# GpSimd's large operations given to VectorE and ScalarE in a hybrid recurrent layer; ScalarE evicts every channel tile

## The chip, the cores and the metric

The kernel runs on one core of a Trainium2 chip. The metric is the time of one execution in microseconds of device time. Three runs of the kernel before took 653.14, 647.74 and 653.92 us; the median is 653.14 us.

## What is computed

One decoder layer is applied to a prompt of 1024 tokens and to a sample group of 64 tokens (8 sequences of 8), 1088 token columns in all. The input is projected once, `z = x @ w_in` (1024 wide), and the columns of z feed four branches of width 256 each:

```
A  RG-LRU:          causal conv of width 4, two sigmoid gates, h = a*h + sqrt(1-a^2)*(gate*x)
B  Mamba-2 SSD:     conv, SiLU, chunked scan, + D*x, gated RMSNorm
C  Gated DeltaNet:  conv, SiLU, l2-normed q and k, triangular solve per chunk, state per chunk, RMSNorm
D  S5:              16 groups of a 64-dim complex diagonal state, GELU, GLU
mix = concat(A, B, C, D), each times its SiLU gate
y   = LayerNorm(alpha * x + mix @ w_out) = (v - mean) * rstd * ln_g + ln_b
```

The outputs are y and the new states of the branches. All values are fp32; the large products are built from a high and a low part of each operand, so that every product is three matmuls.

## The kernel before

The token columns lie on the free axis, channels on the 128 partitions. Engines: TensorE (PE) does matmuls and transposes, VectorE (DVE, `V` in the code, with `tt`, `ts`, `stt` for its operations), ScalarE (ACT, `act`), GpSimd (POOL, `G`), SyncE (SP) issues nearly all DMAs. The kernel is written with generators: `merge` mixes streams by weights, and a planner of the framework then lays down, at compile time, the order of the instructions on each engine. It mostly follows the order of the text, and lets a later instruction pass where an earlier one would still be waiting. On the chip each engine works through its own order.

The stages, in the order of the text:

- `u_tiles` splits x into high and low parts and projects S5's input; `gemm_tok` (from L391) projects the token-wise columns: per 128 tokens 24 matmuls into a bank, ScalarE's eviction (L403), ScalarE's tanh, VectorE's L407 and a DMA of the result to DRAM (L408).
- `s5` (L448) works in two halves, `hf` 0 and 1, of four state pairs each. For each half: `table` (L623) builds powers of the unit rotation by doubling, seven steps of a complex multiplication `cmul` (L455, lines 463 to 465) that is six operations; `outs` (L610) builds the output weights `lo` with six operations on 128x512 (L618 to L620); `half_run` (L636) multiplies the chunk sums by the table (two `cmul` of 128x512), runs eight scans (L650), forms the states `H`, and has TensorE apply `lo` to `H` (L676) and the lag matrix to the inputs (L672). `table(0)` runs on VectorE; `table(1)` and both `outs` run on GpSimd. The temporaries `cm` share four buffers between VectorE and GpSimd.
- Channel tiles of 128 channels: `gemm_strip` (L246) loads a weight tile, ScalarE rounds its high part (L156), VectorE forms the low part (L157), and `gemm_block` (L221) makes three blocks of token columns, 24 matmuls each (L226 to L228), into one of two banks of the pool `pg`. `copy_out` (L239) evicts a block: three calls of four go to ScalarE (L242), the fourth to VectorE (L244). Then `conv` on VectorE (L266) and SiLU (L276 to L279), and GpSimd's small copies of the tails (L270, L271).
- From about 205 us two streams run merged: `gdn` (chunks of 128 tokens: `prep` L787, `invert` L828, `state`, `finish` L990) and `side` (RG-LRU, SSD, the gates, then `project`). In `invert` six levels alternate TensorE (L855, L862, L867), VectorE (L857 and the copies L846 of `spread`) and ScalarE (L864, L868). GpSimd does the decayed keys `kd` (L801), the low part `al` (L839), the decay of the sample states (L966, L1177), SSD's skip `D*x` (L1095), and the square in RG-LRU (L1211).
- `project` (L1382): per 128 tokens two halves of 24 matmuls (L1426 to L1428), VectorE adds alpha*x (L1429) and takes statistics (L1430 to L1435), GpSimd takes the root (L1437), ScalarE normalizes (L1442), GpSimd multiplies by `ln_g` and adds `ln_b` (L1443, L1444, 1024 columns each), and a DMA stores the tile. The last of the nine token tiles takes another way, on VectorE alone (L1448, L1450).

Of the kernel before, what the change touches and what calls it, by code (L numbers as in the profile page):

```python
# [13 lines left out]
AF = mybir.ActivationFunctionType  # L14
OP = mybir.AluOpType
# [37 lines left out]
def hybrid_step(ctx, tc, I, O, dbg=None):  # L53
# [182 lines left out]

    flip = [0]

    def copy_out(dst, src):  # L239
        flip[0] += 1  # L240
        if flip[0] % 4:
            act(dst, src, AF.Copy)  # L242
        else:
            V.tensor_copy(dst, src)  # L244

# [202 lines left out]
    def s5(dp):  # L448
# [161 lines left out]
        def outs(hf):  # L610
# [5 lines left out]
            for j, (u, v) in enumerate((((pa[0], ce[0]), (pa[1], ce[1])), ((pa[0], ce[2]), (pa[1], ce[0])))):  # L616
                x, y = (dt_("cm").rearrange("p (a b c) -> p a b c", a=4, b=8) for _ in range(2))
                G.tensor_tensor(x, *u, OP.mult)  # L618
                G.tensor_tensor(y, *v, OP.mult)
                G.tensor_tensor(lo[:, j], x, y, OP.subtract)  # L620
            return lo.rearrange("p r q t i -> p r q (t i)")

        def table(hf):  # L623

            q0 = 4 * hf
            tab = strip(dp, name="tab")[:, :1024].rearrange("p (r q c) -> p r q c", r=2, q=4)
            for j in range(2):
                (V if hf == 0 else G).tensor_copy(tab[:, j, :, 0], u8[:, j, q0:q0 + 4])
            s = 1
            while s < P:  # L630
                cmul(tuple(tab[:, j, :, s:2 * s] for j in range(2)), tuple(tab[:, j, :, 0:s] for j in range(2)),
                     tuple(tab[:, j, :, s - 1:s].to_broadcast([P, 4, s]) for j in range(2)), [4, s], *((V, V) if hf == 0 else (G, G)))
                s *= 2
            return tab[:, 0], tab[:, 1]
# [105 lines left out]
    def h4(z):  # L740
        return z.rearrange("p (h d) -> p h d", h=4)
# [20 lines left out]
    def gdn(wk, up, q, k, v, rk, rq):  # L762
# [24 lines left out]
        def prep(ti):  # L787
# [12 lines left out]
            kd = r1("kd", "vk", 3)  # L800
            G.tensor_tensor(h4(kd[:n]), h4(kh[:n]), bc(ed[:n, ti], 64), OP.mult)  # L801
            gam = gammas(wk, ti, ac, nac, HO, "i", "g", 2)
# [25 lines left out]
        def invert(d):  # L828
# [9 lines left out]
            for s in blocks:  # L838
                G.tensor_tensor(al[s, :, s], A[s, :, s], ah[s, :, s], OP.subtract)  # L839

# [64 lines left out]
        def state(d):  # L905
# [46 lines left out]
            if ti == 0:  # L952
                for hp in range(2):
# [7 lines left out]
                    for hh in range(2):  # L961
# [3 lines left out]
                        mm(ps[hh * 64:hh * 64 + 64], kd[:NS, h * 64:(h + 1) * 64], wm[:NS].rearrange("p b v -> p (b v)"), start=True, stop=True)  # L965
                    G.tensor_tensor(S0[hp], S0[hp], bc(els, 64), OP.mult)  # L966
                    tt(S0[hp], S0[hp], ps.rearrange("p (b v) -> p b v", b=8), OP.add)
# [73 lines left out]
    def ssd(wk, up, x, BT, CT):  # L1041
# [17 lines left out]
        def chunk(ti):  # L1059
# [34 lines left out]
            y = r1("y")  # L1094
            G.tensor_tensor(h4(y)[:n], h4(xt)[:n], bc(hv[:n, 16:20], 64), OP.mult)  # L1095
            tt(y[:n], py[:n, :256], y[:n], OP.add)
# [68 lines left out]
        def sample_state(bt, xw, st):  # L1165
            for g in range(2):
# [9 lines left out]
                mm(ps, xw[:NS, g * P:(g + 1) * P], bm[:NS].rearrange("p b n -> p (b n)"), start=True, stop=True)  # L1176
                G.tensor_tensor(st[:, g], st[:, g], bc(els, 64), OP.mult)  # L1177
                tt(st[:, g], st[:, g], ps.rearrange("p (b n) -> p b n", b=8), OP.add)
# [8 lines left out]
    def rglru(wk, up, xc, out):  # L1187
# [9 lines left out]
        for i in range(2):  # L1197
# [12 lines left out]
            q = strip(up, name="aq")  # L1210
            G.tensor_tensor(q[:, :CL], a_[:, :CL], a_[:, :CL], OP.mult)  # L1211
            stt(r[:, :CL], q[:, :CL], 1.0, r[:, :CL], OP.add, OP.mult)
# [169 lines left out]
    def project():  # L1382
# [18 lines left out]
        for i in range(9):  # L1401
# [37 lines left out]
            if i < 8:  # L1439
                nb = small([P, 1], name="nb")  # L1440
                stt(nb[:n], mv[:n, 0:1], -1.0, rs[:n], OP.mult, OP.mult)
                act(y[:n], y[:n], AF.Identity, bias=nb[:n], scale=rs[:n])  # L1442
                G.tensor_tensor(y[:n], y[:n], lnp[0][:n], OP.mult)  # L1443
                G.tensor_tensor(y[:n], y[:n], lnp[1][:n], OP.add)  # L1444
                nc.sync.dma_start(dst, y[:n])
# [87 lines left out]
```

## Time and profile before

| what | value |
|---|---|
| runs | 653.14, 647.74, 653.92 us |
| the profiled execution, its own time | 648.38 us |
| its span, first to last instruction | 646.5 us |
| mean granted TensorE clock | 0.976 of full speed |
| TensorE busy | 589.7 us (91%) |
| VectorE busy | 469.6 us (73%) |
| ScalarE busy | 271.6 us (42%) |
| GpSimd busy | 180.9 us (28%) |

The span is what the trace covers; the execution's own time is 1.9 us more. Busy time of an engine is the union of its instructions, waits excluded. The rows further below are of this one execution.

### The profile page before, as it was taken

To read this page: it belongs to the slowest core of one execution; us is meant where nothing else is said; L and a number is where in the kernel's file an instruction comes from. 1 tells how busy PE (TensorE), PEld (TensorE's weight loads), DVE (VectorE), ACT (ScalarE), POOL (GpSimd) and SP (SyncE) were. 2 spreads that over 40 slices of the span, in tenths; PEclk is the share of its full clock that TensorE was granted. 3 is DMA by queue.
4 is the path that set the end of the run, shared out by engine and by line. 5 is a ranking of instruction groups with operands and counts; after the bars stand their busy time and mean duration, and the time that the engine had idled before them with its cause. 6 is when DMAs were issued, how large, how long until landed. Compare 5 with 4: busy or idle time off the path is not lost.

```text
span 646.5 us, 11718 instructions
## 1 busy us (share of the span) xinstructions
PE 589.7 (91%) x4284; PEld 504.0 (78%) x4284; DVE 469.6 (73%) x1378; ACT 271.6 (42%) x677; POOL 180.9 (28%) x305
## 2 busy tenths in 40 slices
PE   3999699499999999988999999999999796999995
PEld 3999699499999786777888877778777564778884
DVE  5996963782559676899897777868777897754443
ACT  5544235143345244854644434354443752333210
POOL 8313119400101322331502032032030122443633
PEclk9999799889899999999999999999999997999998
DMA  8462113032311010100122021001022511013131
GB/s 288 165 191 63 41 34 86 1 96 59 128 57 55 18 36 33 33 18 19 33 69 68 33 89 66 1 17 43 9 75 78 171 43 49 33 55 113 66 117 78
DMA packets 23929, 44.11 MB, mean 68 GB/s; under 512 B 3073, under 2 KB 10193, under 8 KB 23873
## 3 DMA queue, kind: packets, MB, share of 16 engines
q1 hardware_dynamic: 23696, 42.71, 20.1%
q8 instruction: 33, 0.54, 0.4%
q0 software_dynamic: 176, 0.67, 0.3%
q14 instruction: 24, 0.19, 0.1%
HBM read 32.97 MB, written 10.41 MB: 67 GB/s over the span
## 4 chain that ended last, share of the span: by engine, by line
PE 66%; DVE 19%; POOL 5%; issue 5%; ACT 2%; DMA 1%; SPq 0%; DVEq 0%; ACTq 0%; POOLq 0%
PE pg L226 8%; PE pg L227 8%; PE pg L228 8%; PE pg L1428 5%; PE pg L1427 5%; PE pg L1426 5%; DVE tb L846 2%; DVE yb L846 2%; DVE acc L266 2%; PE ssq L755 1%; PE pg L398 1%; DMA x<-in_x_t_dram 1%; PE pg L399 1%; PE pg L400 1%; PE kq L817 1%
## 5 line engine op out<-in xcount | busy, mean ns | idle before, releaser
L226 PE MATMUL pg<-xh,wh 128*128 128x384 f32 (+1 forms) x432 | 150.2, 348 | 9.0 <-DVE z L244 9.0
L227 PE MATMUL pg<-xl,wh 128*128 128x384 f32 (+1 forms) x432 | 149.0, 345 | 0.0
L228 PE MATMUL pg<-xh,wl 128*128 128x384 f32 (+1 forms) x432 | 147.0, 340 | 0.0
L226 PEld LDWEIGHTS pg<-xh,wh 128*128 128x128 f32 x432 | 82.8, 192 | 12.5 <-DVE z L244 9.3
L227 PEld LDWEIGHTS pg<-xl,wh 128*128 128x128 f32 x432 | 82.6, 191 | 2.1 <-issue 0.5
L228 PEld LDWEIGHTS pg<-xh,wl 128*128 128x128 f32 x432 | 82.4, 191 | 1.3 <-issue 0.3
L1426 PE MATMUL pg<-woh,wh 128*128 128x512 f32 (+1 forms) x144 | 58.2, 404 | 1.9 <-ACT wh L1415 1.9
L1427 PE MATMUL pg<-wol,wh 128*128 128x512 f32 (+1 forms) x144 | 58.5, 406 | 0.2
L1428 PE MATMUL pg<-woh,wl 128*128 128x512 f32 (+1 forms) x144 | 57.9, 402 | 0.4 <-DVE wl L1416 0.4
L266 DVE SCALAR_TENSOR_TENSOR acc<-z,pcol,acc 128x1112 f32<-128x1112 f32 x36 | 49.6, 1381 | 5.1 <-ACT acc L264 4.8
L864 ACT ACTIVATE XY<-XY 128x256 f16<-128x256 f32 (+1 forms) x51 | 19.4, 381 | 53.8 <-PE XY L862 48.2
L156 ACT ACTIVATE wh<-wr 128x512 fp32r<-128x512 f32 (+1 forms) x40 | 25.2, 633 | 35.0 <-PE pg L227 28.3
L1429 DVE SCALAR_TENSOR_TENSOR y<-y,pg 128x512 f32<-128x512 f32 (+1 forms) x18 | 12.3, 686 | 32.2 <-PE pg L1428 28.4
L1426 PEld LDWEIGHTS pg<-woh,wh 128*128 128x128 f32 (+1 forms) x144 | 26.6, 184 | 8.9 <-ACT wh L1415 2.2
L1428 PEld LDWEIGHTS pg<-woh,wl 128*128 128x128 f32 (+1 forms) x144 | 26.6, 185 | 7.3 <-DVE wl L1416 0.9
L1427 PEld LDWEIGHTS pg<-wol,wh 128*128 128x128 f32 (+1 forms) x144 | 26.5, 184 | 7.2 <-DVE wol L1393 1.0
L157 DVE TENSOR_TENSOR wl<-wr,wh 128x512 fp32r<-128x512 f32 (+1 forms) x40 | 28.2, 704 | 2.8 <-ACT wh L156 2.4
L857 DVE TENSOR_TENSOR T<-T,lev 128x256 f16<-128x256 f32 (+1 forms) x51 | 21.4, 419 | 10.7 <-PE T L855 10.1
L868 ACT ACTIVATE XY<-XY 128x256 f16<-128x256 f32 (+1 forms) x51 | 19.4, 381 | 22.5 <-PE XY L867 22.5
L242 ACT ACTIVATE z<-pg 128x384 f32<-128x384 f32 (+2 forms) x37 | 14.0, 389 | 34.5 <-PE pg L228 33.2
L846 DVE COPY tb<-T 64x256 f16<-64x256 f16 x99 | 26.2, 264 | 1.6
L846 DVE COPY yb<-XY 64x256 f16<-64x256 f16 x99 | 23.8, 240 | 4.4 <-ACT XY L868 3.0
(453 smaller groups left out, 1398.0 us busy)
## 6 DMA issues: line engine op xcount, KB each, us to landing
wr<-in_w_tiles_dram SPq DMA_DIRECT2D x40, 256.0 KB, 2.9
x<-in_x_t_dram SPq DMA_DIRECT2D x8, 544.0 KB, 6.3
wo<-in_w_out_dram SPq DMA_DIRECT2D x16, 256.0 KB, 2.9
y<-in_x_dram SPq DMA_DIRECT2D x8, 512.0 KB, 3.3
out_y_dram<-y SPq DMA_DIRECT2D x7, 512.0 KB, 2.6
bgd<-bg SPq DMA_DIRECT2D x9, 128.0 KB, 1.8
dud<-us SPq DMA_DIRECT2D x2, 544.0 KB, 4.2
U<-dud SPq DMA_DIRECT2D x16, 68.0 KB, 3.4
```

Of the source, the lines that this page charges most:

```text
L156: act(hv_, wv, AF.Copy)
L157: lo_eng[0].tensor_tensor(lv, wv, hv_.bitcast(F32), OP.subtract)
L226: mm(o, whi[k], xh[:, k, a:b], start=(k == 0), stop=False)
L227: mm(o, whi[k], xl[:, k, a:b], start=False, stop=False)
L228: mm(o, wlo[k], xh[:, k, a:b], start=False, stop=(k == 7))
L266: stt(acc[:, :CL], s[:, j:j + CL], col(wkey, j * nt + i), acc[:, :CL], OP.mult, OP.add)
L846: V.tensor_copy(dst[s, :, s], src[s])
L857: tt(t_[:n], pt[:n], lev[:n, l].unsqueeze(1).to_broadcast([n, 4, 64]), OP.mult)
L864: act(XY[:n, :256], px[:n, :256], AF.Copy)
L1426: mm(ps[:n], mh[k_], woh[:, k_, e], start=(k_ == 0), stop=False)
L1427: mm(ps[:n], mh[k_], wol[:, k_, e], start=False, stop=False)
L1428: mm(ps[:n], ml[k_], woh[:, k_, e], start=False, stop=(k_ == 7))
```

## The change

`copy_out` always uses ScalarE. Operations of GpSimd go to VectorE: S5's output weights and the second half's table, the low part `al`, the two decays of the sample states, and LayerNorm's multiplication and addition, in halves of 512 columns. Others go to ScalarE: the decayed keys `kd` and the skip `D*x`, each as four `Copy` activations of 64 columns with a scale per partition in place of one operation on 256 columns, and the square of RG-LRU. GpSimd keeps the small powers (L999, L1130, L1437), memsets, masks and tail copies. No DMA is added or taken away.

```diff
     def copy_out(dst, src):
-        flip[0] += 1
-        if flip[0] % 4:
-            act(dst, src, AF.Copy)
-        else:
-            V.tensor_copy(dst, src)
+        act(dst, src, AF.Copy)
...
     # s5, outs
-                G.tensor_tensor(x, *u, OP.mult)
-                G.tensor_tensor(y, *v, OP.mult)
-                G.tensor_tensor(lo[:, j], x, y, OP.subtract)
+                tt(x, *u, OP.mult)
+                tt(y, *v, OP.mult)
+                tt(lo[:, j], x, y, OP.subtract)
...
     # s5, table
-                (V if hf == 0 else G).tensor_copy(tab[:, j, :, 0], u8[:, j, q0:q0 + 4])
+                V.tensor_copy(tab[:, j, :, 0], u8[:, j, q0:q0 + 4])
...
-                     tuple(tab[:, j, :, s - 1:s].to_broadcast([P, 4, s]) for j in range(2)), [4, s], *((V, V) if hf == 0 else (G, G)))
+                     tuple(tab[:, j, :, s - 1:s].to_broadcast([P, 4, s]) for j in range(2)), [4, s])
...
     # gdn, prep
-            G.tensor_tensor(h4(kd[:n]), h4(kh[:n]), bc(ed[:n, ti], 64), OP.mult)
+            for h in range(4):
+                act(h4(kd)[:n, h], h4(kh)[:n, h], AF.Copy, scale=ed[:n, ti, h:h + 1])
...
     # gdn, invert
-                G.tensor_tensor(al[s, :, s], A[s, :, s], ah[s, :, s], OP.subtract)
+                tt(al[s, :, s], A[s, :, s], ah[s, :, s], OP.subtract)
...
     # gdn, state, and likewise ssd, sample_state
-                    G.tensor_tensor(S0[hp], S0[hp], bc(els, 64), OP.mult)
+                    tt(S0[hp], S0[hp], bc(els, 64), OP.mult)
...
     # ssd, chunk
-            G.tensor_tensor(h4(y)[:n], h4(xt)[:n], bc(hv[:n, 16:20], 64), OP.mult)
+            for h in range(4):
+                act(h4(y)[:n, h], h4(xt)[:n, h], AF.Copy, scale=hv[:n, 16 + h:17 + h])
...
     # rglru
-            G.tensor_tensor(q[:, :CL], a_[:, :CL], a_[:, :CL], OP.mult)
+            act(q[:, :CL], a_[:, :CL], AF.Square)
...
     # project
-                G.tensor_tensor(y[:n], y[:n], lnp[0][:n], OP.mult)
-                G.tensor_tensor(y[:n], y[:n], lnp[1][:n], OP.add)
+                for e in (slice(0, 512), slice(512, 1024)):
+                    tt(y[:n, e], y[:n, e], lnp[0][:n, e], OP.mult)
+                    tt(y[:n, e], y[:n, e], lnp[1][:n, e], OP.add)
```

## Rows read from the trace of the kernel before

**Rows 1.** The page, part 1: busy time, share, instructions.

```profile
PE 589.7 (91%) x4284; PEld 504.0 (78%) x4284; DVE 469.6 (73%) x1378; ACT 271.6 (42%) x677; POOL 180.9 (28%) x305
```

**Rows 2.** Waits of TensorE: waiter, releaser: total us, times, longest us.

```profile
PE pg L226 <- DVE z L244: 9.0, 1, 9.0
PE XY L862 <- DVE yb L846: 6.6, 5, 5.0
PE pg L398 <- ACT bg L403: 5.8, 1, 5.8
...
PE XY L867 <- ACT XY L864: 0.4, 2, 0.2
```

**Rows 3.** Stretches: length, busy us (instructions) of each engine, granted clock, DMA.

```profile
72.10:76.00 3.90, 3.90 (x17) 3.90 (x18) 3.90 (x12) 1.45 (x7) 0.00 (x0) 0.51 0.10 34
...
129.70:134.50 4.80, 4.78 (x16) 4.78 (x17) 4.80 (x11) 0.29 (x2) 0.00 (x0) 0.55 0.00 0
...
265.00:345.00 80.00, 74.45 (x613) 64.70 (x612) 71.05 (x161) 45.83 (x102) 21.70 (x43) 1.00 0.11 35
...
538.70:546.00 7.30, 7.29 (x47) 5.44 (x48) 4.33 (x15) 1.53 (x4) 0.00 (x0) 0.67 0.36 108
...
572.00:640.00 68.00, 66.78 (x287) 53.48 (x285) 27.40 (x80) 15.28 (x41) 32.31 (x18) 1.00 0.23 85
```

**Rows 4.** Timeline, VectorE, 50 to 90 us: start, length, operation, [idle <-releaser].

```profile
51.79 0.23 DVE L628 COPY tab<-u 128x4 f32<-128x4 f32 x2
...
60.78 1.17 DVE L465 TENSOR_TENSOR tab<-cm,cm 128x256 f32<-128x256 f32 x1
64.39 1.53 DVE L463 TENSOR_TENSOR cm<-tab,G 128x512 f32<-128x512 f32 x1 [2.43 <-POOL lo L620]
...
69.36 0.41 DVE L407 SCALAR_TENSOR_TENSOR bg<-bg 128x256 f32<-128x256 f32 x1
```

**Rows 5.** Timeline, GpSimd, 88 to 142 us.

```profile
96.02 0.31 POOL L628 COPY tab<-u 128x4 f32<-128x4 f32 x2
```

**Rows 6.** Timeline, VectorE, 88 to 142 us.

```profile
117.15 1.53 DVE L463 TENSOR_TENSOR cm<-tab,G 128x512 f32<-128x512 f32 x1 [10.38 <-POOL lo L620]
...
128.65 0.68 DVE L465 TENSOR_TENSOR H<-cm,cm 128x512 f32<-128x512 f32 x1
...
134.98 0.68 DVE L157 TENSOR_TENSOR wl<-wr,wh 128x512 fp32r<-128x512 f32 x1
```

**Rows 7.** Timeline, TensorE, 128 to 147 us.

```profile
129.72 0.69 PE L226 MATMUL pg<-xh,wh 128*128 128x384 f32 x1 [8.96 <-DVE z L244]
...
135.96 0.63 PE L672 MATMUL y<-U,tz 128*128 128x136 f32 x4
...
141.16 0.42 PE L226 MATMUL pg<-xh,wh 128*128 128x320 f32 x1
```

**Rows 8.** Waits of ScalarE.

```profile
ACT z L276 <- DVE hs L465: 12.9, 1, 12.9
```

**Rows 9.** Timeline, GpSimd, 524 to 572 us.

```profile
533.57 2.33 POOL L1443 TENSOR_TENSOR y<-y,ln 64x1024 f32<-64x1024 f32 x1 [1.54 <-ACT y L1442]
```

**Rows 10.** Timeline, VectorE, 524 to 572 us.

```profile
533.49 2.51 DVE L846 COPY tb<-T 64x256 f16<-64x256 f16 x2
...
541.38 0.46 DVE L846 COPY yb<-XY 64x256 f16<-64x256 f16 x2
```

**Rows 11.** Groups by form, VectorE: shapes, count, busy us, mean ns.

```profile
L463 DVE TENSOR_TENSOR cm<-bk 128x512 f32<-128x512 f32 x4 | 2.7, 684 | 0.0
...
L892 DVE TENSOR_TENSOR x<-XY,F 64x256 f32<-64x256 f16 x8 | 3.3, 412 | 0.1
```

**Rows 12.** Groups by form, ScalarE.

```profile
L944 ACT ACTIVATE qd<-ks,ea 128x64 f32<-128x64 f32 x28 | 6.5, 311 | 1.0 <-DVE R L941 1.0
...
L242 ACT ACTIVATE z<-pg 128x256 f32<-128x256 f32 x3 | 1.1, 377 | 0.0
```

**Rows 13.** Groups by form, GpSimd.

```profile
L801 POOL TENSOR_TENSOR kd<-kh,ed 128x256 f32<-128x256 f32 x8 | 7.2, 906 | 42.7 <-DVE kh L798 15.6 <-DVE oss L997 13.7 <-DVE R L941 13.3
```

More of the change, by code (lines that the diff above doesn't have):

```diff
@@ L235, in gemm_ch @@
             yield 3.7
-    flip = [0]
     def copy_out(dst, src):
-        flip[0] += 1
-        if flip[0] % 4:
-            act(dst, src, AF.Copy)
-        else:
-            V.tensor_copy(dst, src)
+        act(dst, src, AF.Copy)
     def gemm_strip(c0, key, i, pool):
@@ L1176, in sample_state @@
                 mm(ps, xw[:NS, g * P:(g + 1) * P], bm[:NS].rearrange("p b n -> p (b n)"), start=True, stop=True)
-                G.tensor_tensor(st[:, g], st[:, g], bc(els, 64), OP.mult)
+                tt(st[:, g], st[:, g], bc(els, 64), OP.mult)
                 tt(st[:, g], st[:, g], ps.rearrange("p (b n) -> p b n", b=8), OP.add)
```

## The prediction

> **What bounds the kernel now.** The page's first part comes first: TensorE is busy 91% of the span, VectorE 73%, ScalarE 42%, GpSimd 28% [rows 1]. TensorE bounds, so only what takes away its idle time or its lowered clock moves the end; GpSimd's busy time by itself buys nothing. TensorE's own waits are therefore the second view. Apart from the start of the kernel, three of them are long: 9.0 us for VectorE's eviction L244, 5.0 of 6.6 us for the copies `yb`, 5.8 us for ScalarE's `bg` [rows 2]. Behind each of them the granted clock is at the lower of its two levels (1.2 GHz of 2.4) for a while: 3.9 us at a mean of 0.51, 4.8 us at 0.55, 7.3 us at 0.67 [rows 3]. That is 1.9, 2.2 and 2.4 us lost on top, so the three places cost 7.7, 11.2 and 7.4 us, 26.3 in all.
>
> The timelines tell where each comes from. First place: VectorE waits 2.43 us for GpSimd's `lo` and then runs a product in 1.53 us; L407, whose store frees the `bg` buffer that ScalarE and after it TensorE wait for, stands behind, at 69.36 us [rows 4]. Second place: GpSimd begins the second table at 96.02 us [rows 5]. VectorE idles 10.38 us for its `lo`, runs S5's second half from 117.15 us to the end of `H` at 129.33, and only then comes L244 [rows 6], for which TensorE has waited 8.96 us [rows 7]. Third place: GpSimd's LayerNorm product starts at 533.57 us [rows 9]; a pair of copies that VectorE runs in 0.46 us elsewhere takes 2.51 us there [rows 10], and the next pair lies under GpSimd's addition.
>
> **The second stretch of S5, part by part.** VectorE takes over the table. The first table, on VectorE already, ran from 51.79 to 61.95 us, partly against GpSimd [rows 4]: 10.2 us is the upper end, and I take 8.5, since its last operation took 1.17 us where a 512-column one takes 0.68. The output weights are six operations of 0.684 us [rows 11], 4.1 us. So 12.6 us come onto VectorE, which idled 10.38 us in one piece there. If the table keeps its place, it begins at 96.0; of the 21.1 us until 117.15, at most 10.7 were other work. With all of that in front, S5's run begins at 119.3, with none of it at 108.6. I take 116, nearer to the late end, since convolutions of VectorE lie there and what was not idle in one piece was mostly work. The run itself is 12.2 us, and its first product needs 0.68 and not 1.53, the second likewise: 10.5. `H` is ready at 126.5, 2.8 us sooner.
>
> TensorE no longer waits for L244: ScalarE evicts that block in 0.377 us [rows 12]. The third block starts at 120.8, takes 6.2 less 2.2 us (129.72 to 135.96 [rows 7], at full clock) and ends at 124.8. Next in TensorE's order are the products with `H`, 5.2 us [rows 7], from 126.5 to 131.7. The next weight tile's low part ended at 135.66 [rows 6], 6.3 us after `H`; now 132.8. So the next tile starts at 132.8 in place of 141.16, a gain of 8.4. Late next is VectorE with `H` and the low part. Ends: 0, if the eviction again stands behind something on its new engine; 11.2, all of the place.
>
> **The first stretch.** The 2.43 us of waiting go, and the slowed operations around them; an estimate of the latter is 3.3 us (1.53 to 0.68 in one product, the like in three more). 4.1 us of output weights come in. L407 comes 1.6 us sooner. In the second stretch VectorE sets the time, so TensorE's gain here counts only as far as VectorE is sooner too: 1.6 us, ends 0 and 7.7.
>
> **LayerNorm.** Eight tiles, each four operations of 0.684 us on VectorE, 2.7 us in place of GpSimd's two. In the projection's steady part TensorE works 66.78 of 68 us and VectorE 27.4 [rows 3]; six tiles there add 16.4 us to VectorE, and TensorE's products still cover them. Without the cover each tile would cost its 2.7 us. Tile 0 lies within the last chunks of the delta-rule stream, at the third place: the 5.0 us wait becomes one of about 2.7 us, if the four operations are put ahead of the copies. Gain 2.3; ends 0 and 7.4 (wait and clock). VectorE's four operations wait for ScalarE's normalization, which waits for GpSimd's root; behind them on VectorE are the copies of `spread`, for which TensorE's next level waits.
>
> By the Trainium skill, SBUF — State Buffer, section Who interferes with whom, GpSimd and a VectorE copy contend for one shared port pair, which the first holds for its whole instruction. That is what the 2.51 us beside GpSimd's 2.33 us show; by the rule alone, with both GpSimd operations gone and VectorE's own taken as hidden, this term would be an estimated 4.7 us.
>
> **The smaller moves.** `al`: 17 operations of 64x256; the nearest row has 0.412 us [rows 11], so 7.0 us more on VectorE. It is needed only at the end of `invert`, and TensorE's levels cover it; ends 0 and +7.0. From 265 to 345 us VectorE is the tightest, 71.05 of 80 us busy [rows 3]; about four `al` (1.6 us) come there, and some evictions leave. I take +0.5. The four decays are 2.7 us on VectorE, followed only by a state's store: 0, end +2.7. The remaining evictions, some 17 of 0.377 us, put 6.4 us on ScalarE: 0. The two squares are at most 1.6 us each on ScalarE (four times an eviction of 256 columns): 0, ends 0 and +3.2. `kd` and `D*x`: 9 chunks, eight activations each, 72 of 0.311 us [rows 12], 22.4 us on ScalarE (1.24 per operation where GpSimd took 0.906 [rows 13]). ScalarE's load rises from 42% to about 47%, so only the order can hurt: `kd` takes its wait for `kh` along, 15.6 us in four chunks on GpSimd [rows 13], and behind it on ScalarE stand the evictions of `XY`, for which TensorE's levels wait. TensorE waits 0.4 us for these now [rows 2]. I take +1; ends 0 and +38 (22.4 + 15.6).
>
> **Sum.** -8.4 - 1.6 - 2.3 + 0.5 + 1 = -10.8, call it -11. The profiled execution took 648.4 us, of which the span is 646.5 and 1.9 lie around it; so 637.4. It lies 4.8 us under the median of the three runs, whose spread is 6.2; I add half of the 4.8: **640 us**. Own range of this case: 631 to 647.
>
> **Rivals.**
> *The evictions wait on ScalarE.* In the same stretch ScalarE stood 12.9 us at L276, which needs VectorE's convolution [rows 8]. If the planner puts the moved eviction behind L276, TensorE waits as before, and VectorE, with 12.6 us more against 10.4 idle, gives nothing back. The S5 terms are 0, and the rest is -0.8: 650. For it: the wait is there and ends after L244 did. Against it: eviction and L276 belong to tiles of different age, and in the trace before ScalarE had evictions of the same block in front of L276. The Trainium skill, PSUM — Partial Sum Buffer, section Engine vs sequencer instructions, calls the queues of ScalarE, VectorE and GpSimd strict FIFO; the 12.9 us agree, and by that rule everything placed behind L276 waits as long.
> *ScalarE becomes the gate of the inversion (slower).* The place is `prep` beside `invert`: `kd` in order ahead of `XY`. Its price is up to 38 us; half of it against the -12.3 of the gains leaves +6.7, 657 us. It decides from the point where more than a third of the 38 us falls on TensorE's levels. For it: GpSimd could wait at no cost and ScalarE can't. Against it: ScalarE is idle over half the time, and TensorE has other streams to work on.
> *All three stalls go.* If the planner fills VectorE's gaps from 80 us on, nearly all of the 26.3 us return, less 1.5: 648.4 - 24.8 + 2.4 = 626.
> *The change does nothing*, since GpSimd's time was off the path: the waits of VectorE for `lo` speak against it; it would look like the first rival.
>
> **Chances.** Forecast 0.55, evictions waiting 0.22, slower 0.15, all stalls gone 0.08. The measurement tells about 1% (6.5 us) from no change. Faster: 0.50 of the first and 0.08, 0.58. Slower: 0.14 of the slow case and 0.03 of the waiting one, 0.17. Same: 0.25. The range takes in the first two cases, most of the fast one and the slow one's half price: 624 to 660.
>
> **What would show it.** Right: TensorE's waits for L244 and for `lo`'s followers are gone, and the granted clock near 72 and 130 us stays up; `H` of the second half lands some 3 us sooner; no copy L846 takes over 1 us beside a LayerNorm operation; VectorE near 500 us busy, GpSimd near 70. Wrong: a wait of TensorE at 120 us for ScalarE's L242; waits of L862 and L867 for ScalarE's `XY` in place of 0.4 us; tiles of the projection further apart than now, with TensorE waiting for L1416 or L1429.

## The result: 634.9 us, faster, and the profile after

The changed kernel takes 634.88 us (median of 4 runs, 631.94 to 635.67) where the kernel before takes 653.26 beside it; the ratio is 0.975, 95% interval 0.970 to 0.980. Measured again on another chip it was 0.967 (0.961 to 0.972). Of all executions reported here one is left out of its ratio, one of the six of F1 below, which took 3126 us at full clock. So the change is faster, and a little more than I forecast. The profiled execution took 631.94 us (span 630.1) against 648.38: 16.4 us less, where my sum was 11.

The changed kernel's line numbers are 3 to 6 lower than those of before: L397 is the L403 of before, L401 the L407, L457 to L459 the `cmul`, L612 to L614 `outs`, L238 the eviction, L841 the copies, L1411 the high parts of the projection (L1415 before), L1440 and L1441 LayerNorm's affine part.

First the page's busy line, which answers to [rows 1]: VectorE and ScalarE took over 14.9 and 22.4 us, GpSimd lost 102.

```profile
PE 591.5 (94%) x4284; PEld 503.6 (80%) x4284; DVE 484.5 (77%) x1469; ACT 294.0 (47%) x769; POOL 78.7 (12%) x192
```

The waits of TensorE in the changed kernel, against [rows 2]: the 9.0 us for L244 are gone, the 5.8 us for `bg` are 2.6, the longest for `yb` is 1.5 and no longer 5.0. Two have grown by a microsecond or more: `wh` of the projection (its high parts), 1.9 us before, now 2.9, and the transposes' wait for `y` of the chunked scan (L1131), 0.6 us before, now 2.8 in four pieces; 1.6 us for the gated unit's inputs (L712, L713) are new. ScalarE's `XY` still costs 0.4.

```profile
PE XY L857 <- DVE yb L841: 3.1, 5, 1.5
PE pg L1422 <- ACT wh L1411: 2.9, 1, 2.9
...
PE pg L392 <- ACT bg L397: 2.6, 1, 2.6
...
PE XY L862 <- ACT XY L859: 0.4, 2, 0.2
```

The 1.5 us for `yb` are not at LayerNorm but in the delta-rule stream, at 283 us. Where LayerNorm cost 5.0 us, the longest is 0.44:

```profile
283.57 0.29 PE L857 MATMUL XY<-T,yb 128*128 128x64 f16 x4 [1.48 <-DVE yb L841]
...
535.18 0.29 PE L857 MATMUL XY<-T,yb 128*128 128x64 f16 x4 [0.44 <-DVE yb L841]
```

The same kernel's stretches (length; busy us of PE, PEld, DVE, ACT, POOL; granted clock; DMA), against [rows 3]. The first place still has a lowered clock (0.62); the second and the third run at 1.00; the steady projection has VectorE at 40.66 of 68 us, and its token tiles start 11.2 us apart, as before.

```profile
67.70:72.00 4.30, 4.30 (x24) 4.30 (x25) 4.30 (x15) 1.39 (x7) 0.00 (x0) 0.62 0.09 30
116.00:122.00 6.00, 6.00 (x39) 5.87 (x39) 6.00 (x17) 1.77 (x4) 0.13 (x1) 1.00 0.00 0
...
530.00:540.00 10.00, 9.56 (x86) 7.13 (x84) 9.53 (x34) 4.42 (x15) 0.00 (x0) 1.00 0.24 71
556.00:624.00 68.00, 65.60 (x282) 52.28 (x280) 40.66 (x105) 15.26 (x40) 4.13 (x7) 1.00 0.23 86
```

VectorE's timeline in the first place, against [rows 4]: the product with the table starts 0.7 us sooner, takes 0.69 and not 1.53, and L401, whose store frees the `bg` buffer, comes after two operations of S5's run, where five stood in front of it before.

```profile
63.69 0.69 DVE L457 TENSOR_TENSOR cm<-tab,G 128x512 f32<-128x512 f32 x1
64.29 0.69 DVE L458 TENSOR_TENSOR cm<-tab,G 128x512 f32<-128x512 f32 x1
64.89 0.42 DVE L401 SCALAR_TENSOR_TENSOR bg<-bg 128x256 f32<-128x256 f32 x1
```

VectorE in the second place, against [rows 5, 6]. The table starts at 99.08 and S5's run at 110.36, with nothing but S5's own work and one low part (L157) between; `H` is complete at 120.6 (129.3 before), and the first half of the next weight tile's low part is ready eleven microseconds ahead of it. The second half comes at 125.01, 5 us behind `H`.

```profile
99.08 0.24 DVE L622 COPY tab<-u 128x4 f32<-128x4 f32 x2
...
109.16 0.68 DVE L157 TENSOR_TENSOR wl<-wr,wh 128x512 fp32r<-128x512 f32 x1
109.76 0.68 DVE L614 TENSOR_TENSOR lo<-cm,cm 128x512 f32<-128x512 f32 x1
110.36 0.68 DVE L457 TENSOR_TENSOR cm<-tab,G 128x512 f32<-128x512 f32 x1
...
119.91 0.69 DVE L459 TENSOR_TENSOR H<-cm,cm 128x512 f32<-128x512 f32 x1
...
125.01 0.68 DVE L157 TENSOR_TENSOR wl<-wr,wh 128x512 fp32r<-128x512 f32 x1
```

TensorE there, against [rows 7]: the products with `H` follow the channel blocks without a gap, and the next tile starts at 126.32 (141.16 before).

```profile
121.12 0.63 PE L666 MATMUL y<-U,tz 128*128 128x136 f32 x4
...
126.32 0.41 PE L226 MATMUL pg<-xh,wh 128*128 128x320 f32 x1
```

ScalarE evicts the blocks of that stretch at once, none behind the SiLU of [rows 8]:

```profile
112.95 0.50 ACT L238 ACTIVATE z<-pg 128x64 f32<-128x64 f32 x2 [1.33 <-PE pg L228]
117.14 0.49 ACT L238 ACTIVATE z<-pg 128x384 f32<-128x384 f32 x1 [3.69 <-PE pg L228]
```

VectorE at LayerNorm's first tile, against [rows 9, 10]: its own affine operations, 0.68 us each and the first two in one piece, alternate with the copies of `spread`, and every pair of copies takes about 0.46 us.

```profile
524.55 1.28 DVE L1440 TENSOR_TENSOR y<-y,ln 64x512 f32<-64x512 f32 x2
525.76 0.47 DVE L841 COPY yb<-XY 64x256 f16<-64x256 f16 x2
526.25 0.42 DVE L852 TENSOR_TENSOR T<-T,lev 128x256 f16<-128x256 f32 x1
526.60 0.68 DVE L1441 TENSOR_TENSOR y<-y,ln 64x512 f32<-64x512 f32 x1
527.20 0.45 DVE L841 COPY tb<-T 64x256 f16<-64x256 f16 x2
```

**Where the time goes, place by place.** The table gives the start of the same TensorE matmul in every profiled execution, as the difference to before in us, read from the timelines: the first and the last token-wise product (L398 of before), the last product with `H` (L676), the last of the gated unit, the last norm product of the channel tiles, the 64th `J` (`J` are the last matmuls of each chunk's inversion, 16 in a chunk), the first product of the first and of the second token tile of the output projection (the 1st and 17th of L1426), the last `J`, the last product of the projection. Each execution starts with an offset of its own (first column).

```
                    tok0   tokN   H      unit   norm   J64    proj0  proj16  Jlast  projN
before              36.4   82.4  141.0  162.5  191.0  376.9  508.8   526.3  556.1  637.9
the change          -0.2   -4.7  -14.8  -12.4   -9.2  -11.4  -10.2    -7.5  -13.4  -16.3
the change, again    0.3   -4.1  -14.3  -12.0  -12.0  -14.3  -13.2   -10.2  -16.1  -19.1
evict alone         -0.2   -0.3   -6.0   -1.9   -0.3    1.4    2.2     3.0    2.9    2.8
S5 alone            -1.6   -5.5  -13.1  -11.4  -11.3  -11.2  -11.2    -9.6   -9.3   -9.3
S5, output weights   0.6   -5.4   -8.2   -8.2   -8.1   -7.9   -7.9    -7.9   -8.3   -8.3
LayerNorm alone      0.5    0.7    0.8    0.8    0.8    0.8    0.8     0.8   -4.9   -6.9
LayerNorm, POOL too -1.8   -1.9   -2.1   -2.1   -2.1   -2.0   -2.0    -2.0   -7.6    3.9
small moves alone    0.9    1.3    1.5    1.5    3.0   -0.9   -0.8     2.5    0.7    0.6
S5 + LayerNorm       1.1   -5.0  -11.0   -8.8   -7.2   -7.0   -7.0    -5.5  -11.1  -13.2
all but evict       -1.3   -5.4  -11.5   -9.0   -7.4  -11.3  -11.2    -7.8  -13.4  -16.4
all but small        1.0   -5.1  -15.2  -13.1  -11.5   -9.8   -8.9    -8.3  -14.0  -16.1
first tile on DVE    1.1   -4.9  -15.1  -12.7  -11.1  -13.4  -10.6   -13.7  -18.3  -22.0
unit's weights too   0.5   -5.5  -15.7  -14.2  -14.5  -17.8   -9.0   -12.6  -17.3  -21.0
```

"The change, again" is F4 below, "LayerNorm, POOL too" G4, and the two last lines G3 and H1. The changed kernel gains 4.5 us in the first place (4.7 less its own offset of 0.2), 10.1 in the second, loses 5.6 of that by 191 us, gains 1.0 through the delta-rule stream, loses 2.7 at the first projection, and gains 8.8 from LayerNorm's first tile to the end, 5.9 of them by the last `J`.

### The profile page after: what moved, and what is told of

It is laid out like the page before. It is cut to its first block, busy times and chain, and to the rows that moved or that the text cites. A ratio compares the mean times of both kernels' runs of the same rounds, so it can differ in the third digit from the quotient of the medians.

```text
span 630.1 us, 11770 instructions
## 1 busy us (share of the span) xinstructions
PE 591.5 (94%) x4284; PEld 503.6 (80%) x4284; DVE 484.5 (77%) x1469; ACT 294.0 (47%) x769; POOL 78.7 (12%) x192
## 4 chain that ended last, share of the span: by engine, by line
PE 52%; DVE 21%; issue 4%; ACT 4%; POOL 2%; DMA 1%; SPq 1%; DVEq 0%; ACTq 0%; POOLq 0%
PE pg L226 6%; PE pg L228 6%; PE pg L227 6%; PE pg L1424 4%; PE pg L1423 4%; PE pg L1422 4%; DVE acc L260 3%; DVE yb L841 2%; DVE T L852 1%; PE ssq L749 1%; DVE tb L841 1%; PE rg L1199 1%; PE cb L1077 1%; DVE wl L157 1%; PE yd L1088 1%
## 5 line engine op out<-in xcount | busy, mean ns | idle before, releaser
L228 PE MATMUL pg<-xh,wl 128*128 128x384 f32 (+1 forms) x432 | 148.5, 344 | 0.0
L1422 PEld LDWEIGHTS pg<-woh,wh 128*128 128x128 f32 (+1 forms) x144 | 26.4, 183 | 10.2 <-ACT wh L1411 3.4
L238 ACT ACTIVATE z<-pg 128x384 f32<-128x384 f32 (+2 forms) x48 | 17.5, 395 | 32.7 <-PE pg L228 31.1
L157 DVE TENSOR_TENSOR wl<-wr,wh 128x512 fp32r<-128x512 f32 (+1 forms) x40 | 27.4, 688 | 4.8 <-ACT wh L156 4.6
L863 ACT ACTIVATE XY<-XY 128x256 f16<-128x256 f32 (+1 forms) x51 | 19.5, 382 | 14.8 <-PE XY L862 14.5
L841 DVE COPY yb<-XY 64x256 f16<-64x256 f16 x99 | 21.8, 221 | 4.5 <-ACT XY L863 2.9
L1425 DVE SCALAR_TENSOR_TENSOR y<-y,pg 128x512 f32<-128x512 f32 (+1 forms) x18 | 12.3, 682 | 15.3 <-PE pg L1424 15.3
L392 PE MATMUL pg<-wh,xh 128*128 128x268 f32 x72 | 21.4, 298 | 2.6 <-ACT bg L397 2.6
```

What stands on the lines that cost most here:

```text
L157: lo_eng[0].tensor_tensor(lv, wv, hv_.bitcast(F32), OP.subtract)
L228: mm(o, wlo[k], xh[:, k, a:b], start=False, stop=(k == 7))
L392: mm(o, xh[:, k, c0:c0 + P], whi[k], start=(k == 0), stop=False)
L841: V.tensor_copy(dst[s, :, s], src[s])
L1422: mm(ps[:n], mh[k_], woh[:, k_, e], start=(k_ == 0), stop=False)
```

## The experiments

My theory: the gain is made in three places, by S5 and LayerNorm leaving GpSimd, and the small moves are worth nothing. The rivals: the eviction alone does the second place; the whole is a general relief of VectorE from GpSimd; the small moves or the eviction hold it back.

**E1, the eviction alone.**

```diff
-    flip = [0]
-
     def copy_out(dst, src):
-        flip[0] += 1
-        if flip[0] % 4:
-            act(dst, src, AF.Copy)
-        else:
-            V.tensor_copy(dst, src)
+        act(dst, src, AF.Copy)
```

> Of the change only the eviction is made: ScalarE evicts all channel tiles; S5, LayerNorm and the small moves stay on GpSimd. Theory of three places: the third block of the second stretch no longer waits 9 us for L244, but the products with H still wait for H at 129.3 us, so the next weight tile starts about 5 us sooner (136 instead of 141.2); the first and the third place stay as they were. About 643 us in a profiled run of 648, a ratio near 0.992. Rival, the eviction alone made the gain of the second stretch: the whole 10 us, ratio 0.984. Rival, S5 alone made it: ratio 1.000.

Measured: 1.0022 (0.9996 to 1.0048), no gain. TensorE, in this kernel's timeline, runs its third block without a wait and then stands for `H`, as expected:

```profile
127.84 0.50 PE L670 MATMUL y<-H,lo 64*128 64x136 f32 x4 [2.69 <-DVE H L459]
129.22 0.50 PE L670 MATMUL y<-H,lo 64*128 64x136 f32 x4 [0.88 <-DVE H L459]
```

The next tile is 6.0 us sooner, and all of it is gone 50 us later: TensorE waits 2.0 us for the gated unit's rounded weights and inputs, and then runs from 150 to 170 us at a granted clock of 0.85 (its stretch):

```profile
150.00:170.00 20.00, 18.03 (x107) 17.25 (x106) 6.79 (x14) 9.58 (x20) 0.25 (x2) 0.85 0.15 61
```

So the first expectation held up to 141 us and failed after it.

**E2, S5 alone** (output weights and second table on VectorE, the diff of `outs` and `table` that stands ahead).

> Of the change only S5 is made: output weights and second table on VectorE. Every fourth channel tile is still evicted by VectorE; LayerNorm and the small moves stay on GpSimd. Theory of three places: the first place returns its 4.7 us, H comes near 121 us, and what is left of the second place is that the eviction of one block still stands behind S5's run on VectorE, about 3 us; 4.7 + 7, of which about 5 are given back by the gated unit's weights at 141 us and by a lowered clock between 150 and 180 us: about 641, ratio 0.989. Rival, the eviction alone made the gain of the second stretch: only the first place returns, and VectorE's longer list delays the eviction: 645, ratio 0.995 to 1.00.

Measured: 0.9845 (0.9809 to 0.9882), the largest single part. `tokN` -5.5, `H` -13.1, of which 11.3 stay up to the first projection and 9.3 to the end. With VectorE still evicting every fourth tile, TensorE no longer waits for L244; what is left in that place is this:

```profile
PE y L676 <- DVE H L465: 1.9, 1, 1.9
```

So S5's edit alone gives 3.9 of the 4.5 us of the first place (its offset of -1.6 taken out) and 7.6 of the 10.1 us of the second. My expectation that some 3 us of the wait for the eviction would stay was wrong.

**E3, LayerNorm alone** (its product and addition on VectorE, in halves).

> Of the change only LayerNorm's product and addition are made by VectorE, in halves; all else stays as before. Theory of three places: the pairs of copies at 533 and 541 us go back to 0.46 us each, TensorE's wait of 5.0 us for them goes, and so does the stretch of lowered clock: 7.4 to 8.8 us, about 640, ratio 0.987, and nothing differs up to 510 us. Rival, my prediction's sum: 2.3 us, ratio 0.996, since VectorE's four operations stand in front of the copies. Rival, the projection pays for VectorE's longer list: the tiles after 560 us come over 7.0 us apart.

Measured: 0.9877 (0.9832 to 0.9921). Nothing differs until 526 us, then 7.7 us are gained by the last projection. The stretch that holds it, in the kernel before and in this one: TensorE 9.97 and 13.74 of 15 us busy, clock 0.77 and 1.00.

```profile
530.00:545.00 15.00, 9.97 (x65) 7.19 (x64) 11.47 (x31) 3.42 (x7) 5.39 (x3) 0.77 0.18 54
```

```profile
530.00:545.00 15.00, 13.74 (x117) 9.44 (x117) 13.99 (x52) 5.93 (x16) 0.72 (x1) 1.00 0.19 54
```

**E4, the small moves alone** (`al` and decays to VectorE; `kd`, `D*x` and the square to ScalarE).

> Of the change only the small moves are made: al, the states' decays on VectorE; kd, D*x and the gate's square on ScalarE. S5, LayerNorm and the evictions stay as before. Theory of three places: nothing, ratio 0.998 to 1.002; the waits of L862 and L867 for ScalarE's XY stay near 0.4 us. Rival, GpSimd's instructions slow VectorE everywhere and freeing it is worth some microseconds all over the delta-rule stream: ratio 0.992 to 0.995, with the gain growing steadily from 260 to 500 us. Rival, ScalarE's kd holds up the inversion: ratio 1.003 or more.

Measured: 0.9938 (0.9910 to 0.9966), a gain that I had not expected; the profiled execution, 648.75 us, is one of the longest of its twelve (644.4 to 649.5), so its trace shows less than the times. It gains 3.9 us between the norms and the 64th `J`, in one place rather than steadily. From 260 to 300 us, in the kernel before and in this one (VectorE 36.42 and 34.95 of 40 us, TensorE 35.37 and 38.54), and GpSimd less (12.58 and 7.92):

```profile
260.00:300.00 40.00, 35.37 (x266) 30.14 (x265) 36.42 (x79) 25.96 (x50) 12.58 (x26) 1.00 0.09 28
```

```profile
260.00:300.00 40.00, 38.54 (x299) 32.97 (x298) 34.95 (x78) 30.80 (x60) 7.92 (x23) 1.00 0.09 28
```

One of the moved operations can be seen to hold VectorE there. In the kernel before, a pair of copies lies beside GpSimd's square (L1211) and takes 2.19 us; in E4, with the square on ScalarE, the pair of the same place takes 0.45:

```profile
281.65 2.08 POOL L1211 TENSOR_TENSOR aq<-acc 128x1112 f32<-128x1112 f32 x1
281.62 2.19 DVE L846 COPY tb<-T 64x256 f16<-64x256 f16 x2
```

```profile
282.08 0.45 DVE L847 COPY tb<-T 64x256 f16<-64x256 f16 x2
```

And it gives 3.3 us back at the first projection, where TensorE now waits 4.0 us for ScalarE (1.9 us in the kernel before):

```profile
PE pg L1428 <- ACT wh L1417: 4.0, 1, 4.0
```

**F1 to F4, the parts in company**, on one chip: S5 and LayerNorm; the change without its eviction; without its small moves; the change itself.

> S5 and LayerNorm go to VectorE as in the change; the eviction by turns and the small moves stay as before. Theory of two places: the gains of the two single edits add up, 0.9845 x 0.9877 = 0.972, about 632 us, as fast as the whole change. Rival, the second place needs the eviction too: 637 or more. Rival, the small moves carry their own 0.6% in any company: 0.972, and the kernels that have them are 4 us faster than this one.

> The change without its eviction: VectorE still evicts every fourth channel tile, all else as in the change. Theory: the single edits multiply, 0.9845 x 0.9877 x 0.9938 = 0.966, some 5 us under the whole change, since the eviction alone was 1.0022. Rival, the second place needs the eviction: slower than the whole change by 3 us or more, TensorE waiting for L244 near 120 us. Rival, the small moves gain nothing once S5 and LayerNorm are moved: 0.972, the same as without them.

> The change without its small moves: al, kd, D*x, the decays and the gate's square stay on GpSimd; S5, LayerNorm and the eviction as in the change. Theory that the single edits multiply: 0.9745 to 0.975, some 4 us slower than the whole change if that is measured at 0.969, from the stretch between 200 and 510 us. Rival, my prediction's sum (the small moves at +1.5 us): 1 to 2 us faster than the whole change.

> The changed kernel itself again, beside its parts on one chip. The product of the four single edits is 0.9845 x 0.9877 x 0.9938 x 1.0022 = 0.968; the first measurement gave 0.975 (0.970 to 0.980). If it comes near 0.975 again, the parts do not add up, and some 4 us of their gains are lost when they are put together.

Measured, in this order: 0.9705 (0.9658 to 0.9752), 0.9690 (0.9650 to 0.9730), 0.9718 (0.9682 to 0.9754), 0.9668 (0.9614 to 0.9721). S5 and LayerNorm together give what the whole gives; the eviction and the small moves move it by 0.5% at most, less than the intervals. The product of the four single edits, 0.968, lies in the interval of the second measurement and just under that of the first, so nothing shows a loss in putting them together. The traces tell more than the times. Between the norms and the first projection (`norm` and `proj0` of the table) the small moves gain 3.8 us in both kernels that have them without the eviction; the eviction costs 2.5 and 2.6 in both that have it without them; with both, the change's two executions gain 1.0 and 1.2 (G3 and H1, which have both as well, lose 0.5 and 5.5; for H1 see there). Between the first and the seventeenth projection the executions with the small moves lose 2.7 to 3.4, those without them 0 to 1.6 (but for the two last lines, which mend that place). And the eviction's own gain is in the second place (`tokN` to `H`): 10.1 to 10.2 us with S5's edit and the eviction, 6.0 to 7.6 with S5's edit and without it. Each of the two gives back most of what it gains.

**G2, half of S5's edit**: both output weights on VectorE, the second table still on GpSimd.

```diff
-                G.tensor_tensor(x, *u, OP.mult)
-                G.tensor_tensor(y, *v, OP.mult)
-                G.tensor_tensor(lo[:, j], x, y, OP.subtract)
+                tt(x, *u, OP.mult)
+                tt(y, *v, OP.mult)
+                tt(lo[:, j], x, y, OP.subtract)
```

> The kernel before with one half of the S5 edit: both output weights on VectorE, the second table still on GpSimd. Theory: the first place needs only the output weights, since its table was on VectorE already, so the token-wise products end 4 to 5 us sooner, as with the whole S5 edit; in the second place GpSimd begins its table where it did and has only that to make, so VectorE waits less long for it, and part of the rest returns: 642 to 646 where the whole S5 edit gave 0.9845. Rival, the first place moved for another reason (a start that differs from run to run): the token-wise products end where they did.

Measured: 0.9878 (0.9833 to 0.9923). The first place is whole (-5.4 at `tokN`, -6.0 against its own start); the second returns 2.8 of 7.6 us. VectorE now waits for the table, and TensorE for L244:

```profile
105.78 0.69 DVE L618 TENSOR_TENSOR cm<-bk,s5p 128x512 f32<-128x512 f32 x1 [4.45 <-POOL tab L465]
```

```profile
PE pg L226 <- DVE z L244: 5.7, 1, 5.7
```

**G4, LayerNorm on VectorE, and GpSimd busy beside it.** As E3, with two operations of GpSimd per tile whose result is not used.

```diff
+        spare = strip(up, name="spare")[:, :1024]
...
+                G.tensor_tensor(spare[:n], lnp[0][:n], rs[:n].to_broadcast([n, 1024]), OP.mult)
+                G.tensor_tensor(spare[:n], spare[:n], lnp[1][:n], OP.add)
                 for e in (slice(0, 512), slice(512, 1024)):
                     tt(y[:n, e], y[:n, e], lnp[0][:n, e], OP.mult)
                     tt(y[:n, e], y[:n, e], lnp[1][:n, e], OP.add)
```

> LayerNorm's product and addition are made by VectorE, and GpSimd makes two operations of the same size beside them, into a tile that nobody reads. No instruction waits for GpSimd's two. Theory of the slowed copies: GpSimd's work itself slows VectorE's copies beside it, so pairs of copies of over 1 us are back near 530 us and most of the 7 to 8 us that the move alone gained are lost: ratio 0.995 to 1.00. Rival, the gain came from what no longer waits for GpSimd (the stores of y, the buffers of y): ratio 0.9877 as with the move alone, no copy over 1 us.

Measured: 1.0118 (1.0073 to 1.0163). It was not the test that I had planned: the planner put GpSimd's sixteen operations late, one behind the other from 604.5 us, beside the projection and not beside the copies at 530 us, which stay short; up to the last `J` this kernel gains 5.6 us there, as E3 does (5.7). So the third place itself was not tried with a busy GpSimd. What it shows is what such a run does to VectorE. GpSimd's first two:

```profile
604.53 1.89 POOL L1444 TENSOR_TENSOR spare<-ln,rs 64x1024 f32<-64x1024 f32 x1 [6.23 <-DVE wl L1417]
606.50 2.52 POOL L1445 TENSOR_TENSOR spare<-spare,ln 64x1024 f32<-64x1024 f32 x1
```

VectorE beside them:

```profile
604.16 0.49 DVE L1417 TENSOR_TENSOR wl<-gate,wh 128x128 fp32r<-128x128 f32 x2 [0.48 <-ACT wh L1416]
604.58 2.20 DVE L1417 TENSOR_TENSOR wl<-z,wh 128x128 fp32r<-128x128 f32 x2
606.80 0.69 DVE L1430 SCALAR_TENSOR_TENSOR y<-y,pg 128x512 f32<-128x512 f32 x1
607.40 1.78 DVE L1417 TENSOR_TENSOR wl<-z,wh 128x128 fp32r<-128x128 f32 x1
609.10 0.68 DVE L1431 BATCH_NORM_STATS2 bn<-y 128x6 f32<-128x512 f32 x1
...
616.03 2.34 DVE L1442 SCALAR_TENSOR_TENSOR nb<-mv,rs 128x1 f32<-128x1 f32 x1 [0.44 <-POOL rs L1438]
619.73 3.89 DVE L1447 TENSOR_TENSOR y<-y,ln 128x512 f32<-128x512 f32 x2 [1.36 <-ACT y L1443]
```

A low part of 128x128 takes 1.78 us where it takes 0.28 elsewhere, LayerNorm's products some 1.95 each (3.89 for two) and not 0.68, a 128x1 operation 2.34 and not 0.16. L1430, which has one operand in PSUM, and the statistics, which have a single operand, keep their 0.69 us. In these rows the held operations take 1.4 to 2.6 us whatever their size, about as long as GpSimd's beside them (1.9 to 2.7). GpSimd's root for the next tile also stands behind the run, and TensorE ends up waiting 11.5 us for L1430: this kernel's loss is both together.

**G3, the first projection's high parts on VectorE**, on top of the whole change.

```diff
-                    act(h_[:, k_], m, AF.Copy)
+                    V.tensor_copy(h_[:, k_], m) if i == 0 else act(h_[:, k_], m, AF.Copy)
```

> The changed kernel, with the eight high parts of the first token tile of the output projection (L1411) rounded by VectorE and no longer by ScalarE. Theory that they stand behind five roundings of output weights and kd's four activations on ScalarE: TensorE's wait of 2.9 us near 500 us falls under 1 us, the lowered clock behind it (0.63 to 0.66 over 6 us) mostly goes, and the stretch that lost 2.7 to 3.0 us against before loses less than 1: ratio 0.962 to 0.965 where the change had 0.967. Rival, the output weights themselves come late there: TensorE waits as long, for them, and the ratio stays.

The place, in the trace of the change measured again (ScalarE's timeline): the high parts of `z`, whose inputs have long been there, stand behind five roundings of output weights, and TensorE waits 2.94 us for them.

```profile
498.49 2.72 ACT L1388 ACTIVATE woh<-wo 128x512 fp32r<-128x512 f32 x5
501.09 0.71 ACT L1411 ACTIVATE wh<-z 128x64 fp32r<-128x64 f32 x4
```

With the edit, TensorE at the first projection, and the stretch behind it (granted clock 0.63 before the edit, over the same 6 us):

```profile
498.12 0.44 PE L1422 MATMUL pg<-woh,wh 128*64 128x512 f32 x1 [0.17 <-DVE wh L1411]
```

```profile
502.00:508.00 6.00, 5.73 (x36) 3.14 (x35) 5.17 (x11) 4.52 (x11) 0.00 (x0) 1.00 0.76 253
```

Measured: 0.9661 (0.9614 to 0.9707). In the trace the place costs nothing any more (-10.6 to -13.7, a gain of 3.1 where the change loses 3.0). In the times it is not told apart from the 0.9668 of the change itself.

**H1, the gated unit's weights loaded ahead of the reloads**, on top of G3.

```diff
+            if hf:
+                glu_.append(strip(dp, name="glu")[:, :512].rearrange("p (k f) -> p k f", k=2))
+                nc.sync.dma_start(glu_[0], I["s5_glu_w"].rearrange("(k p) f -> p k f", p=P))
             nc.sync.dma_start(yd_d[hf], ys)
...
+        glu_ = []
...
-        glu = strip(dp, name="glu")[:, :512].rearrange("p (k f) -> p k f", k=2)
-        nc.sync.dma_start(glu, I["s5_glu_w"].rearrange("(k p) f -> p k f", p=P))
+        glu = glu_[0]
```

> As the kernel before it (the change, with the first token tile's high parts on VectorE), and the weights of S5's gated unit are loaded ahead of the second half's store and its eight reloads on SyncE's queue, no longer behind them. Theory that part of the second stretch's gain is given back there: ScalarE rounds these weights and the first half's columns before 135 us, TensorE's waits for gh and gl (1.6 us near 142 us) go, TensorE is no longer idle 1.6 of 10 us there, and the lowered clock of 150 to 170 us (0.84 and 0.81, about 3.5 us) mostly goes too: 2 to 5 us, ratio 0.959 to 0.963 where it was 0.966. Rival, the lowered clock there has another origin (it differs from run to run): about 1.5 us, 0.964. Rival, the unit's products, now earlier, take TensorE's time from the channel tiles and only change places: 0.966.

Measured: 0.9631 (0.9582 to 0.9679). The stretch behind the unit, without and with the edit, at 0.83 and at 1.00 of the clock:

```profile
150.00:170.00 20.00, 20.00 (x121) 19.78 (x120) 11.39 (x36) 9.01 (x19) 3.38 (x15) 0.83 0.38 136
```

```profile
150.00:170.00 20.00, 19.77 (x139) 19.51 (x139) 14.33 (x38) 9.21 (x22) 3.86 (x16) 1.00 0.41 147
...
460.00:470.00 10.00, 10.00 (x38) 8.14 (x38) 3.10 (x10) 1.47 (x5) 0.94 (x2) 0.50 0.16 52
```

I had expected TensorE's wait for the unit's rounded weights and inputs to go; 1.2 of 1.6 us are left, now at 134 us. What goes is the lowered clock: from 150 to 177 us the mean is 1.00 here and 0.81 to 0.94 in each of the thirteen other profiled executions, 0.94 in the kernel before. 3.4 us are gained by 191 us and 4.4 by the 64th `J`; then the profiled execution loses them again, at half clock from 460 to 470 us and some time on both sides. Ahead of it TensorE waited 1.28 us for `y` of the chunked scan, at 457 us; the execution without the edit has the same wait of 1.27 us at 461 us, both of the change have one of 1.28, and all three keep 1.00. Its six runs lie between 623.7 and 629.5 us at mean clocks of 0.992 to 0.979. This is the fastest version by ratio; whether it beats the change is not shown (0.963 with an end at 0.968, against 0.967 with an end at 0.961).

## Why the prediction was right, and where its steps were not

The forecast was right in sign and its range held the time: 640 us for 634.9, with the likeliest case's own range from 631 to 647. The offset between profiled execution and median came out as taken (2.9 us for 2.4). That the total comes within 5 us is in part luck: the three places gave 23.4 us where I had 12.3, and about 7 us were given back elsewhere where I had 1.5.

**The second place, -8.4, measured -10.1.** The path up to `H` was nearly right: it was forecast 2.8 us sooner than before, and came 4.0 sooner when the 4.7 by which `tokN` came sooner are taken out (129.3 to 120.6). The step that failed is the next tile's low part, which I let end 6.3 us behind `H` and hold up the tile. Its first half was done at 109.84; its second ended at 125.69, still 5.1 us behind `H`, but before the tile began, which it did when the products with `H` ended. In the kernel before it was no different (135.66 and 141.16), so the low part was not a term of the path. And my reading of the cause was too wide: the eviction, which I held to be needed there, gave nothing at the end by itself (E1), and S5 alone took TensorE's wait for L244 away (E2); with the eviction 2.5 to 4.2 us more come in that place, and where it has no small moves beside it 2.5 go again between the norms and the first projection.

**The first place, -1.6, measured -4.5.** The sum treated L407 as standing last in its row of operations. Of the 4.5 us by which it came sooner, 0.7 are the earlier start, 2.0 the two products at 0.69 us, and 1.8 its place: three operations of 0.6 us now stand behind it. The planner's order behind the product is another one when the product is not held up. G2 shows that the output weights alone do it. The sign that the clock stays up near 72 us did not come true: TensorE still waits 2.6 us for `bg`, and the clock is at 0.62 behind it.

**LayerNorm, -2.3, measured -8.8 (E3: -7.7).** The step that failed is "if the four operations are put ahead of the copies". They alternate with them, and TensorE's longest wait for `yb` in this place falls to 0.44 us rather than 2.7; I also left the lowered clock of 2.4 us in the sum, and it went with the wait (E3: 1.00 from 530 to 545 us). The upper end, 7.4, was the nearer value; 5.9 us of the 8.8 are there by the last `J`. The other 2.9 (E3: 2.0) were no term of the sum: in the kernel before TensorE waits 2.0 us in all for VectorE between 560 and 572 us, in the change 0.85; the rest of them is not accounted for. The Trainium skill, SBUF — State Buffer, section Who interferes with whom, would have given an estimated 4.7 for the wait and was the better guide. It also says that a VectorE instruction with at most one SBUF input, outside the 2-port modes, does not contend with GpSimd, and that one with two SBUF inputs contends with a GpSimd instruction that reads SBUF. G4's rows agree: 0.69 us for L1430 and the statistics, 1.78 for a low part that takes 0.28. The copies of `spread` have one input and were held all the same (2.51 us for 0.46, [rows 10]); in which mode they run no row shows.

**The small moves, +1.5, measured as a gain**: 0.6%, some 4 us, alone in E4; in company 2.3 us at the end of the trace (F4 against "all but small": -19.1 and -16.1, less 0.7 between their offsets), with ratios of 0.9668 and 0.9718, whose intervals overlap. `al` was sized right (0.420 us each for 0.412), and the inversion did not wait for ScalarE: 0.4 us as before, so the slower rival's mechanism is absent. Two things were missing. Between 260 and 300 us, where VectorE is the tightest, I counted only what came onto it; its busy time fell all the same (36.42 to 34.95 us in E4), and TensorE gained 3 to 4 us there. The square on GpSimd held a pair of copies for 2.19 us, as LayerNorm's product did in the third place; how much of the gain is that, was not tried operation by operation. And ScalarE's longer list does stand in the way, but at the first projection's high parts, a wait of 1.9 us that I had not listed: 2.7 to 3.4 us go there, and G3 takes them back. In the change the wait is 1.0 us longer, and behind it the clock falls (0.66 from 504.5 to 509.5 us), which it does not in the kernel before. `kd`'s four activations (1.06 us at 496.5) lie in that list; that they are the whole of it is argued, not shown.

**What the sum did not contain** is that a gain can be returned: the gated unit's weights lay behind eight reloads on SyncE's queue, so TensorE, sooner there, waited and then ran at a lowered clock (-14.8 to -9.2 in the profiled execution, to -12.0 in the second). H1, with the load moved, is the one profiled execution without the lowered clock, so the place of the load is shown to matter, by one execution; why the clock stays up there though 1.2 us of the wait are left is not shown.

**The rivals.** *Evictions wait on ScalarE*: no, the blocks are evicted at 112.95 and 117.14 with no wait behind the SiLU. *All stalls go*: its list of places was right (4.5, 10.1 and 8.8 of 7.7, 11.2 and 7.4), and what was returned kept it from its 626; G3's and H1's medians, with their further edits and on other chips, reach it (626.7 and 626.9). *The change does nothing*: no.

**Left open.** Why the clock is lowered after a wait of 1.3 us at 457 us in one execution and not in another is not shown; nor how much of E4's 0.6% is the place at 260 us and how much a better draw of the clock.

## What to carry to other kernels

Before a move is sized by busy time, look at who runs slowed or waits beside the operation that is moved: two edits out of four, the two whose operations VectorE waited for or ran beside on TensorE's path, carried nearly the whole 3%. Follow each gain to the next late thing: a load behind other loads, a rounding behind other roundings; here about a third was given back at two such places, and in the profiled executions each fell to an edit of a few lines, though the times don't tell either from the change. And size a held-up operation with its list, not with its wait alone, since the order behind it changes when the hold goes.

## What was not expected of the hardware

- GpSimd's 1024-column operations (1.9 to 2.7 us) held VectorE's operations with two SBUF operands for about their own length, whatever these operations' size: 0.16 to 2.34 us for 128x1, 0.28 to 1.78 for 128x128. One PSUM operand was enough to escape (0.69 us).
- Executions of one kernel spread by 8.6 us (the change, six runs from 626.2 to 634.8) and follow the mean granted clock (0.993 to 0.977). The same wait of TensorE, 1.3 us for the chunked scan's `y`, was followed by more than 10 us at 1.2 GHz in one execution (H1) and by none in another (G3).
